# Moving operands placed elsewhere relative to their weights, and four joints between stages, in a two-block transformer kernel

## The chip, the cores and the metric

The kernel runs on one core of a Trainium2 chip. The time is that of one launch, in device microseconds (us). Engines are named as in the profile: PE is TensorE (matmuls), PEld its weight loads, DVE is VectorE, ACT is ScalarE, POOL is GpSimd, SP is the engine that issues most transfers (DMAs).

## What is computed

Two transformer blocks in a row on 256 tokens of width 2048, all in float32. Cut to the products that matter here:

```
# first block
p  = rms_norm(h) @ w_in                      # RWKV and sparse attention read p
h += concat(y_rwkv, y_att) @ w_mix_out
h += cross_attention(rms_norm(h) @ w_q, rms_norm(mem) @ w_kv) @ w_o
h += square(relu(rms_norm(h) @ w_up)) @ w_down          # w_up: 2048 x 8192
# second block, with 16 meta tokens ahead
h += mixer(rms_norm(rms_norm(h)) @ w_in_2) @ w_out_2
q  = rms_norm(h) @ w_query_2                 # picks 128 of 16384 experts per token, gates g
h += (g * gelu(rms_norm(h) @ peer_u.T)) @ peer_v        # peer_u, peer_v: 16384 x 2048
```

## The kernel before, in words

**Float32 in three products.** Every weight arrives as a tile `raw` of 128 x 1024 (512 KB, eight blocks of 128 x 128; `half`). ACT copies it to a rounded `whi` (L276, 128 x 512 a time) and DVE subtracts that to give the rest, `wlo` (L261). Each block then takes three matmuls (`linear`, `mm` at L255) into one PSUM tile `plin`: `whi` with the high half of the activations, `whi` with the low half, `wlo` with the high half. The weight block is the stationary operand, which PE loads (one load for each matmul); the activations are the moving operand, 256 columns wide. A column of output takes 16 such blocks, 48 matmuls; `evac` takes it out of PSUM.

**Names of the moving operands.** `xh`/`xl` are the normed input, in the products of w_in, w_kvc and w_mix; `uh`/`ul` the squared MLP activations, in w_down; `ph`/`pl` the pairs made by `pair`, in most other products (w_qc, w_up, w_in2, w_out2, the query and peer_u); `oh`/`ol` the attention output, in w_oc. In peer_v the roles turn: the gated activations `wh`/`wl` are stationary (128 x 128 of them at a time) and `whi`/`wlo` move, 512 columns, into eight PSUM tiles `o` that add up over all 128 groups of experts (`experts_out`).

**Stages, in order:** w_in (with the streams of RWKV and sparse attention driven between its blocks), w_kvc, w_mix, w_qc, w_oc, then w_up and w_down by turns in four parts, w_in2 (with the second block's attention streams), w_out2, the query and its top-k, peer_u, peer_v.

**What sets the order.** A scheduler places the instructions by priority; `half` is marked high priority, and `keep_in_program_order` pins DMAs on SP in program order. At a norm, PE sums squares with a vector of ones (`pcs`), DVE takes the inverse root (`rsv`, `rsh`, `ldr`, `rst`), and PE spreads it to all partitions (`pbc`). `load_norm` (L426) does the first of these and calls `inv_rms` at its end. In w_oc, `norm_tile` (L1107) splits each new column of `h` into `ph` (ACT) and `pl` (DVE), and POOL squares it (`sqt`) and adds it to `acc`. In `experts_out`, group j needs `g<-gd`, a DMA of the gates from the scattered table, then POOL's product with the activations `A`, then `wh` on ACT and `wl` on DVE.

Of the kernel before, what the change touches and what calls it, by code (L numbers as in the profile page):

```python
# [8 lines left out]
F32 = mybir.dt.float32  # L9
# [3 lines left out]
AF = mybir.ActivationFunctionType  # L13
OP = mybir.AluOpType
# [107 lines left out]
NCOL_IN = len(W_COLS)  # L122
# [61 lines left out]
def _layout(inp):  # L184
    a = {k: np.asarray(v) for k, v in inp.items()}
    o = {}
    o["x"] = _tT(a["x"][0])
    o["mem"] = _tT(a["mem"][0])
    o["pos"] = np.ascontiguousarray(a["positions"].reshape(1, S))
    o["vecs"] = _vecs(a)  # L190
    cc = _const_arrays()
    o["ident"] = np.ascontiguousarray(cc["ident"])
    o["iota"] = np.ascontiguousarray(cc["iota"])
    o["consts_a"] = np.ascontiguousarray(np.concatenate([cc[n] for n in CA], 1))
    o["dups"] = np.ascontiguousarray(np.concatenate([cc["dup"], cc["rdup"]], 1)[:64])
# [12 lines left out]
    fl = np.concatenate([w2[:, 7168:], w2[:, 7168:], np.zeros((D, 112), w2.dtype)], 1)  # L208
    qkv = w2[:, :6144].reshape(D, 2, 3, 8, 128).transpose(0, 1, 3, 2, 4).reshape(D, 6144)
    o["w_in2"] = _blocks(np.concatenate([qkv[:, :3072], fl, qkv[:, 3072:], w2[:, 6144:7168]], 1))  # L210
    o["w_out2"] = _blocks(a["w_out_2"][0])
    o["w_pq"] = _blocks(a["peer_w_query_2"][0])
    o["keys"] = np.ascontiguousarray(a["peer_sub_keys_2"][0].reshape(16, NKEY, 128).transpose(2, 0, 1))
    u = a["peer_u_2"][0].reshape(NKEY, NKEY, KT, 128)
    o["pu"] = np.ascontiguousarray(
        u.transpose(1, 3, 2, 0).reshape(NKEY, 128, 2, 8, 128).transpose(0, 2, 1, 3, 4)).reshape(2 * NKEY, 128, 8, 128)
    v = a["peer_v_2"][0].reshape(NKEY, NKEY, 2, 1024)
    o["pv"] = np.ascontiguousarray(v.transpose(1, 2, 0, 3)).reshape(2 * NKEY, 128, 8, 128)
    return o
# [25 lines left out]
class Kernel:  # L245
# [180 lines left out]
    def load_norm(self, src, gain, xh, xl, dst, eps, acc, w, tiles):  # L426

        nc = self.nc
        ts = []
        for q in range(4):  # L430
            t = tiles(q)
            with self.tc.high_priority():
                self.tc.keep_in_program_order(nc.sync.dma_start(t, src[:, 4 * q:4 * q + 4]))
            ts.append(t)
            if q < 2:
                self.ahead.append(self.half(w[len(self.ahead)], True))
            for k in range(4):
                self.split(xh[:, 4 * q + k], xl[:, 4 * q + k], t[:, k], self.v(gain, 4 * q + k))
            if q:
                self.squares(ts[q - 1], acc, q == 1, q == 1)  # L440
        with self.tc.high_priority():
            self.tc.keep_in_program_order(nc.sync.dma_start(self.ident, self.io["ident"]))
        self.squares(ts[3], acc, False)
        self.inv_rms(dst, acc, eps)

    def squares(self, t, acc, first, pool=False):

# [9 lines left out]

    def inv_rms(self, dst, acc, eps):
        r = self.small("ldr")
        with self.tc.high_priority():  # L460
            p = self.colsum([acc[:, 0], acc[:, 1]], S)
            self.rsqrt(r, p[:, 0:2], 1.0 / D, eps)
            self.bcast(dst, r, S)

    def block1(self, c0):
        nc, tc = self.nc, self.tc
# [4 lines left out]
        xp = self.pool("xa", 1, xstack)  # L471
        yp = self.pool("yp", 1, xstack)
        ctx = ExitStack()
        cp = self.pool("ca", 1, ctx)
        ph = self.pool("pa", 1, ctx)
        ca = cp.tile([128, wid], F32, name="ca")
        C = {n: ca[:, o:o + w] for n, (o, w) in off.items()}
        self.C = C
        xh = xp.tile([128, KT, S], F32R, name="xh", tag="xh")
        xl = xp.tile([128, KT, S], F32R, name="xl", tag="xl")  # L480
        rx = ph.tile([128, S], F32, name="rx")
# [63 lines left out]

        def evac(c, p):
            kind, g, q = KIND[c]
            if kind == "dsa":
                self.dsa_evac(g, p)
            elif kind == "rwkv":  # L550
                w, j = divmod(q, 2)
# [6 lines left out]
                shift(c, p, cur["AR"][:, j, 1] if w == 0 else cur["KV"[w - 1]][:, j])  # L558
                if q == 5:
                    rs.append(self.rwkv_group(g, cur["AR"], cur["K"], cur["V"], fr))  # L560
            elif g == 0:
                self.first = shift(c, p, L)
                self.act(th, L[0:64], AF.Tanh)
                ds.append(loads())
                ds.append(low_rank())
                ds.append(self.tables())
            elif g == 1:
                shift(c, p, M)
                self.act(sM[64:96], M[64:96], AF.Sigmoid)
                ds.append(self.dsa_ki())  # L570
            else:
                shift(c, p, XG)
                self.act(XG, XG, AF.Sigmoid)
# [8 lines left out]
        self.ds = (ds, ds2)  # L582

        def dense():
            yield from self.linear(self.io["w_in"], 0, NCOL_IN, KT, xh, xl, S, evac, more=(2,))
            rm = ph.tile([128, S], F32, name="rm")
            kv = self.kv = kvp.tile([128, 8, S], F32, name="kv", tag="kv")

# [16 lines left out]
                    self.squares(tile(c), xacc, c == 0)  # L605

            yield from self.linear(self.io["w_kvc"], 0, 8, KT, xh, xl, S, kv_evac)
            self.inv_rms(rm, xacc, 1e-5)
            for c in range(8):
                self.gtt(kv[:, c], kv[:, c], rm, OP.mult)  # L610

# [506 lines left out]
            self.gtt(acc, acc, t, OP.add)  # L1118

    def rstd(self, acc, dst, eps, dim=D):  # L1120
        p = self.colsum([acc], S)
        r = self.small("rr")
        self.rsqrt(r, p[:, 0:2], 1.0 / dim, eps)
        self.bcast(dst, r, S)
        return r
# [39 lines left out]
    def cross(self, cp, cxh, cxl, rc):  # L1165
# [48 lines left out]

        self.drive(self.linear(self.io["w_qc"], 0, 4, KT, cxh, cxl, S, query), todo, 1, flush=False)
        self.mxh, self.mxl = self.pair(self.xb)
        acc = wk.tile([128, S], F32, name="acc2", tag="acc", bufs=2)

        def out(c, p):
            self.vtt(h[:, c], p, h[:, c], OP.add)  # L1220
            self.norm_tile(c, h[:, c], "norm_mlp", self.mxh[:, c, 0:S], self.mxl[:, c, 0:S], acc, wk)


        first = [self.plin.tile([128, 512], F32, name="plin", tag="plin") for _ in range(2)] + [self.ps("pc"), self.ps("pc")]
# [23 lines left out]
            out(c, first[c][:, 0:S])  # L1248
        self.lin(self.io["w_oc"], 2, KT - 4, 4, oh, ol, S, out, c0=4)
        self.rm = wk.tile([128, S], F32, name="rmlp", tag="rc", bufs=2)  # L1250
        self.rstd(acc, self.rm, 1e-5)

    def mlp(self, up):
        nc, h, wk = self.nc, self.h, self.wk
        U = {}
        g12 = wk.tile([128, KT], F32, name="g12")
        o1, o2 = self.vec["norm_final"][0], self.vec["norm_mix_2"][0]
        self.vtt(g12, self.vecs[:, o1:o1 + KT], self.vecs[:, o2:o2 + KT], OP.mult)
# [54 lines left out]
        p1, p2 = self.colsum([acc1], S), self.colsum([acc2], S)
        r1, m, r2 = self.small("r1"), self.small("m2"), self.small("r2")
        self.rsqrt(r1, p1[:, 0:2], 1.0 / D, 1e-5)
        self.vtt(m, r1, r1, OP.mult)
        self.vtt(m, m, p2[:, 0:2], OP.mult)
        self.rsqrt(r2, m, 1.0 / D, 1e-6)
        self.vtt(r2, r2, r1, OP.mult)
        self.bcast(self.r12[:, NMETA:], r2, S)  # L1320
        r1b = wk.tile([128, S], F32, name="r1b", tag="rc", bufs=2)
        self.bcast(r1b, r1, S)
        for c in range(KT):
            self.gtt(h[:, c], h[:, c], r1b, OP.mult)

    def meta_tokens(self):

# [20 lines left out]
    def block2(self):  # L1348
# [8 lines left out]
        nc.sync.dma_start(ca, self.io["consts_b"])  # L1357
        C = self.C = {n: ca[:, o:o + w] for n, (o, w) in off.items()}
        bxh, bxl, r12 = self.bxh, self.bxl, self.r12
        rs = wk.tile([128, S], F32, name="r12s", tag="rc", bufs=2)  # L1360
        self.ts(rs, r12[:, NMETA:], 128 ** -0.5, None, OP.mult)
        gq = self.small("gq", 1)
        self.ts(gq, self.v("fox_q_gain_2", 0), 128 ** -0.5, None, OP.mult)

# [3 lines left out]
        yh, yl = self.pair(self.pool("xxb", 1, mx, side="right"))  # L1368
        acc_sb = wk.tile([128, S], F32, name="accsb", tag="acc", bufs=2)
        acc_fo = wk.tile([128, S], F32, name="accfo", tag="acc", bufs=2)  # L1370
        s0, s1 = [], []
# [157 lines left out]
        def evac(c, p):  # L1529
            if c == 24:  # L1530
                forget(p)
            elif c < 49:
                hd, w = divmod(c - (c > 24), 3)
                nn, n0 = ((S, NMETA), (SP, 0), (SP, 0))[w]
                t = cur[w] = b2.tile([128, nn], F32, name="qkv"[w] + "_", tag="qkv"[w], bufs=3)
                self.vtt(t, p, rs if c < 24 and w == 0 else r12[:, n0:], OP.mult)
# [24 lines left out]
            self.vtt(h[:, c], p, h[:, c], OP.add)  # L1561
            self.norm_tile(c, h[:, c], "norm_ffn_2", self.pxh[:, c, 0:S], self.pxl[:, c, 0:S], acc, wk)

        self.lin(self.io["w_out2"], 0, KT, KT, yh, yl, S, out)
        self.rf = self.xa.tile([128, S], F32, name="rf")
        self.rstd(acc, self.rf, 1e-6)
        mx.close()
# [192 lines left out]
    def experts_out(self, es):  # L1760
        nc, A, sp = self.nc, self.A, self.sp
        with ExitStack() as c:
# [12 lines left out]
            for j in range(NKEY):  # L1775
                w = A[j // 32][:, j % 32]
                with self.tc.high_priority():
# [4 lines left out]
                        self.tc.add_manual_dep(i.ins, x.ins.name, order if prev else sync, reason="the table is complete")  # L1782
                    prev = i
                    self.gtt(g, w, g, OP.mult)
                    wh, wl = ((sp if j == 0 else vp).tile([128, S], F32R, name=n) for n in ("wh", "wl"))
                    self.split(wh, wl, g)
                for hf in range(2):
                    hi, lo = self.half(self.io["pv"][2 * j + hf])
                    first, last = j == 0, j == NKEY - 1
                    for d in range(2):  # L1790
                        for b in range(2):
# [31 lines left out]
```

## Time and profile before

| what | value |
| --- | --- |
| time, median of 3 runs | 3501.79 us (3500.44 to 3502.34) |
| the profiled execution | 3498.64 us, its span 3496.9 us |
| TensorE's mean granted clock in it | 0.996 of full |
| PE busy | 3451.6 us (99% of the span), 28376 matmuls |
| DVE, ACT, POOL busy | 2298.9, 1762.9, 880.1 us |

The span runs from the first to the last instruction of the profiled execution. A busy engine is one with an instruction under way; matmuls overlap, so how fast they follow each other is read from their starts.

### The profile page before, as it was taken

To read this page: it belongs to the slowest core of one execution; us is meant where nothing else is said; L and a number is where in the kernel's file an instruction comes from. 1 tells how busy PE (TensorE), PEld (TensorE's weight loads), DVE (VectorE), ACT (ScalarE), POOL (GpSimd) and SP (SyncE) were. 2 spreads that over 40 slices of the span, in tenths; PEclk is the share of its full clock that TensorE was granted. 3 is DMA by queue.
4 is the path that set the end of the run, shared out by engine and by line. 5 is a ranking of instruction groups with operands and counts; after the bars stand their busy time and mean duration, and the time that the engine had idled before them with its cause. 6 is when DMAs were issued, how large, how long until landed. Compare 5 with 4: busy or idle time off the path is not lost.

```text
span 3496.9 us, 72405 instructions
## 1 busy us (share of the span) xinstructions
PE 3451.6 (99%) x28376; PEld 3240.5 (93%) x28376; DVE 2298.9 (66%) x4248; ACT 1762.9 (50%) x3187; POOL 880.1 (25%) x788
## 2 busy tenths in 40 slices
PE   8999999999999999999999999999999999999999
PEld 7899889899999999999999999999999888888887
DVE  7678767765656568656557799755555566666666
ACT  5444555554545455444445455555555455555554
POOL 2222213310101015200003002777777011111111
PEclk9999999999999999999999999999999999999999
DMA  5333435476767575544345656777777666666666
GB/s 198 113 119 128 165 124 184 148 218 192 226 190 228 185 230 183 158 145 145 121 133 176 202 180 188 185 186 186 187 187 185 206 210 213 211 213 211 210 214 194
DMA packets 230279, 635.99 MB, mean 182 GB/s; under 512 B 58320, under 2 KB 75408, under 8 KB 229552
## 3 DMA queue, kind: packets, MB, share of 16 engines
q1 hardware_dynamic: 193072, 631.22, 57.5%
q0 software_dynamic: 36864, 0.15, 2.3%
q8 instruction: 222, 3.64, 0.4%
q14 instruction: 121, 0.99, 0.1%
HBM read 610.16 MB, written 21.10 MB: 181 GB/s over the span
## 4 chain that ended last, share of the span: by engine, by line
PE 96%; DVE 2%; DMA 1%; issue 1%; ACT 0%; POOL 0%; DVEq 0%; SPq 0%; ACTq 0%; POOLq 0%
PE plin L255 68%; PE o L255 21%; PE po L255 1%; DVE wlo L261 1%; PE pfz L255 1%; PE pw L255 0%; PE pbc L255 0%; DMA hd<-ht 0%; PE pz L255 0%; PE pix L255 0%; PE pcs L255 0%; PE px L751 0%; PE pt L751 0%; DVE xl L264 0%; PE py L255 0%
## 5 line engine op out<-in xcount | busy, mean ns | idle before, releaser
L261 DVE TENSOR_TENSOR wlo<-raw,whi 128x512 fp32r<-128x512 f32 x2208 | 1602.7, 728 | 959.2 <-ACT whi L276 857.9
L276 ACT ACTIVATE whi<-raw 128x512 fp32r<-128x512 f32 x2208 | 1388.7, 630 | 1445.4 <-PE plin L255 988.5
L255 PE MATMUL plin<-ph,wlo 128*128 128x256 f32 (+1 forms) x4560 | 1290.8, 283 | 2.2 <-DVE wlo L261 2.2
L255 PE MATMUL plin<-pl,whi 128*128 128x256 f32 (+1 forms) x4560 | 1291.0, 283 | 0.0
L255 PE MATMUL plin<-ph,whi 128*128 128x256 f32 (+1 forms) x4560 | 1285.1, 282 | 1.6 <-DVE ut L261 0.7
L255 PEld LDWEIGHTS plin<-ph,wlo 128*128 128x128 f32 x4560 | 863.7, 190 | 4.5 <-DVE wlo L261 2.4
L255 PEld LDWEIGHTS plin<-ph,whi 128*128 128x128 f32 x4560 | 863.4, 189 | 3.0 <-issue 1.6
L255 PEld LDWEIGHTS plin<-pl,whi 128*128 128x128 f32 x4560 | 858.4, 188 | 1.6 <-issue 1.1
L1668 POOL DMA_INDIRECT gd<-GT,EI x256 | 414.7, 1620 | 347.5 <-DMA raw<-in_pu_dram 218.8
L255 PE MATMUL o<-wlo,wh 128*128 128x512 f32 x1024 | 405.8, 396 | 0.0
L255 PE MATMUL o<-whi,wl 128*128 128x512 f32 x1024 | 404.4, 396 | 0.0
L255 PE MATMUL plin<-xh,whi 128*128 128x256 f32 x1136 | 327.9, 289 | 9.0 <-ACT whi L276 8.4
L255 PE MATMUL plin<-xh,wlo 128*128 128x256 f32 x1136 | 327.4, 289 | 4.1 <-DVE wlo L261 3.9
L255 PE MATMUL plin<-xl,whi 128*128 128x256 f32 x1136 | 326.9, 288 | 1.7 <-DVE xl L264 1.7
L255 PE MATMUL o<-whi,wh 128*128 128x512 f32 x1024 | 323.4, 397 | 3.9 <-ACT wh L276 3.9
L255 PE MATMUL plin<-uh,wlo 128*128 128x256 f32 x1024 | 289.7, 283 | 0.0
L255 PE MATMUL plin<-ul,whi 128*128 128x256 f32 x1024 | 289.7, 283 | 0.0
L255 PE MATMUL plin<-uh,whi 128*128 128x256 f32 x1024 | 289.6, 283 | 0.0
L258 POOL TENSOR_TENSOR g<-A,g 128x256 f32<-128x256 f32 x128 | 105.8, 827 | 668.0 <-DMA g<-gd 546.1
L255 PEld LDWEIGHTS o<-whi,wh 128*128 128x128 f32 x1024 | 193.3, 189 | 50.9 <-ACT wh L276 4.1
L255 PEld LDWEIGHTS o<-wlo,wh 128*128 128x128 f32 x1024 | 193.4, 189 | 46.1
L255 PEld LDWEIGHTS o<-whi,wl 128*128 128x128 f32 x1024 | 192.2, 188 | 47.2
(563 smaller groups left out, 3520.4 us busy)
## 6 DMA issues: line engine op xcount, KB each, us to landing
raw<-in_pu_dram SPq DMA_DIRECT2D x256, 512.0 KB
raw<-in_pv_dram SPq DMA_DIRECT2D x256, 512.0 KB
raw<-in_w_in_dram SPq DMA_DIRECT2D x208, 512.0 KB
raw<-in_w_up_dram SPq DMA_DIRECT2D x128, 512.0 KB
raw<-in_w_down_dram SPq DMA_DIRECT2D x128, 512.0 KB
raw<-in_w_mix_dram SPq DMA_DIRECT2D x32, 512.0 KB
gd<-zero SPq DMA_DIRECT2D x64, 256.0 KB
raw<-in_w_out_dram SPq DMA_DIRECT2D x32, 512.0 KB
```

Source lines behind the costliest of these rows:

```text
L255: self.nc.tensor.matmul(out, l, r, start=start, stop=stop)
L258: self.nc.gpsimd.tensor_tensor(out, a, b, op=op)
L261: return self.nc.vector.tensor_tensor(out, a, b, op=op)
L276: return self.nc.scalar.activation(out, a, AF.Copy, **kw)
L1668: i = self.nc.gpsimd.indirect_dma_start(self.gd, bass.IndirectOffsetOnAxis(self.EI[tb][:, s:s + 1], 0), self.GT[tb][:, s:s + 1], None, com ...
```

## The change

**Pads.** Three tiles that nobody writes or reads: `xpad` (64 bytes in each partition) ahead of `xh`/`xl`, `upad` (64 bytes) ahead of `uh`/`ul`, `vpad` (480 bytes) ahead of `wh`/`wl` in peer_v. In the built program the start of `xh` in a partition goes from byte 60256 to 60320, that of `uh` from 54112 to 54176, and that of `wh` from 192896 to 193376 (the first `wh`/`wl`, of j = 0, stand in another pool and are not moved). The blocks of `whi` start at byte 35680 and every 512 bytes after it, since a block is 128 floats wide; `wlo` lies a multiple of 512 further. So the moving operand's start less the weights' start, counted modulo 512 (called its place below), goes from 0 to 64 for `xh`/`xl` and `uh`/`ul`. In peer_v, moving less stationary goes from 480 to 0. The `ph`/`pl` tiles have rows of 1088 bytes, twice 512 and 64, so that the 16 rows of one column of output stand at all eight multiples of 64 in turn, before and after.

**Joints.** (1) At the start, `load_norm` no longer ends with the inverse root; the first three columns of w_in stay in PSUM until the third is done, and then the root is taken and all three are evacuated. (2) In w_oc, ACT squares four columns at once (`hsq`, 128 x 1024) and POOL adds 128 x 512 at a time, where POOL did eight 128 x 256 operations. (3) The end of the MLP becomes a stream of the second block's schedule. (4) w_out2 begins with four columns at once, block row by block row, as its weights are laid out anew. And in `experts_out` the loads of peer_v's first weights are pinned behind the first `g<-gd`.

```diff
 def load_norm(...):
         self.squares(ts[3], acc, False)
-        self.inv_rms(dst, acc, eps)
...
+        xp.tile([128, 16], F32, name="xpad")
         xh = xp.tile([128, KT, S], F32R, name="xh", tag="xh")
...
         def evac(c, p):
             kind, g, q = KIND[c]
-            if kind == "dsa":
+            if c < 3:
+                early.append((c, p))
+                if c == 2:
+                    self.inv_rms(rx, xacc, 1e-5)
+                    for e in early:
+                        lead(*e)
+            elif kind == "dsa":
...
-            yield from self.linear(self.io["w_in"], 0, NCOL_IN, KT, xh, xl, S, evac, more=(2,))
+            yield from self.linear(self.io["w_in"], 0, NCOL_IN, KT, xh, xl, S, evac, more=(2, 3))
...
         def out(c, p):
             self.vtt(h[:, c], p, h[:, c], OP.add)
-            self.norm_tile(c, h[:, c], "norm_mlp", self.mxh[:, c, 0:S], self.mxl[:, c, 0:S], acc, wk)
+            self.split(self.mxh[:, c, 0:S], self.mxl[:, c, 0:S], h[:, c], self.v("norm_mlp", c))
+            if c % 4 == 3:
+                t = cp.tile([128, 4, S], F32, name="hsq", tag="hsq", bufs=2)
+                self.act(t, h[:, c - 3:c + 1], AF.Square)
+                if c == 3:
+                    self.gtt(acc, t[:, 0:2], t[:, 2:4], OP.add)
+                else:
+                    self.gtt(t[:, 0:2], t[:, 0:2], t[:, 2:4], OP.add)
+                    self.gtt(acc, acc, t[:, 0:2], OP.add)
...
     def mlp(self, up):
+        up.tile([128, 16], F32, name="upad")
...
+        def tail():
             p1, p2 = self.colsum([acc1], S), self.colsum([acc2], S)
...
+            yield
             self.bcast(self.r12[:, NMETA:], r2, S)
...
+        self.tail = tail()
...
-        self.lin(self.io["w_out2"], 0, KT, KT, yh, yl, S, out)
+        p = [self.plin.tile([128, 512], F32, name="plin", tag="plin") for _ in range(2)] + [self.ps("pc"), self.ps("pc")]
+        for k in range(KT):
+            if k % 2 == 0:
+                w = self.half(self.io["w_out2"][k // 2])
+            for c in range(4):
+                hi, lo = (self.block(x, 4 * (k % 2) + c) for x in w)
...
+        for c in range(4):
+            out(c, p[c][:, 0:S])
+        self.lin(self.io["w_out2"], 8, KT - 4, KT, yh, yl, S, out, c0=4)
...
+                    if j == 0:
+                        vp.tile([128, 120], F32, name="vpad", bufs=1)
                     wh, wl = ((sp if j == 0 else vp).tile([128, S], F32R, name=n) for n in ("wh", "wl"))
...
-                    hi, lo = self.half(self.io["pv"][2 * j + hf])
+                    hi, lo = self.half(self.io["pv"][2 * j + hf], j == 0)
```

At the start, DVE's order, before: the chain of the inverse root (`rsv` to the last `ldr`) with two weight splits within it.

```order
L261 TENSOR_TENSOR wlo<-raw,whi 128x512 x2
L270 TENSOR_SCALAR rsv<-pcs 128x2
L268 TENSOR_SCALAR rsh<-rsv 128x2
L270 TENSOR_SCALAR ldr<-rsh 128x2
L261 TENSOR_TENSOR rst<-ldr 128x2
L261 TENSOR_TENSOR wlo<-raw,whi 128x512
L264 SCALAR_TENSOR_TENSOR rst<-rst,rsv 128x2
L261 TENSOR_TENSOR wlo<-raw,whi 128x512
L264 SCALAR_TENSOR_TENSOR ldr<-rst,ldr 128x2
L261 TENSOR_TENSOR rst<-ldr 128x2
```

And after:

```order
L262 TENSOR_TENSOR wlo<-raw,whi 128x512 x8
L271 TENSOR_SCALAR rsv<-pcs 128x2
L269 TENSOR_SCALAR rsh<-rsv 128x2
L271 TENSOR_SCALAR ldr<-rsh 128x2
L262 TENSOR_TENSOR rst<-ldr 128x2
L265 SCALAR_TENSOR_TENSOR rst<-rst,rsv 128x2
L265 SCALAR_TENSOR_TENSOR ldr<-rst,ldr 128x2
L262 TENSOR_TENSOR rst<-ldr 128x2
```

The two weight splits now stand ahead of the chain. On PE the four `pcs` and the two `pbc` stay next to each other, behind 144 matmuls of w_in where it was 96.

In w_oc, POOL's order, before: squares and sums of one column each (`acc_9108` is the sum).

```order
L258 TENSOR_TENSOR acc_9108<-h 128x256
L258 TENSOR_TENSOR sqt<-h 128x256 x2
L258 TENSOR_TENSOR acc_9108<-acc_9108,sqt 128x256 x2
L258 TENSOR_TENSOR sqt<-h 128x256
L258 TENSOR_TENSOR acc_9108<-acc_9108,sqt 128x256
```

And after, all of it:

```order
L259 TENSOR_TENSOR acc_9109<-hsq 128x512
L259 TENSOR_TENSOR hsq<-hsq 128x512
L259 TENSOR_TENSOR acc_9109<-acc_9109,hsq 128x512
L259 TENSOR_TENSOR hsq<-hsq 128x512
L259 TENSOR_TENSOR acc_9109<-acc_9109,hsq 128x512
L259 TENSOR_TENSOR hsq<-hsq 128x512
L259 TENSOR_TENSOR acc_9109<-acc_9109,hsq 128x512
```

31 operations of 256 columns became 7 of 512.

Between peer_u and peer_v, ACT's order, before (`A` is the activation of a group of experts, the last of peer_u's work):

```order
L273 ACTIVATE A_34249<-et 128x256
L276 ACTIVATE whi<-raw 128x512 x4
L273 ACTIVATE A_34249<-et 128x256
L276 ACTIVATE wh<-g 128x256 x3
L276 ACTIVATE whi<-raw 128x512 x7
L276 ACTIVATE wh<-g 128x256
```

And after:

```order
L277 ACTIVATE whi<-raw 128x512 x4
L274 ACTIVATE A_34222<-et 128x256 x2
L277 ACTIVATE wh<-g 128x256
L277 ACTIVATE whi<-raw 128x512 x4
L277 ACTIVATE wh<-g 128x256
L277 ACTIVATE whi<-raw 128x512
L277 ACTIVATE wh<-g 128x256
```

The four `whi` that stood between the last two `A` were peer_v's; they now stand behind the last `A` and the first `wh`. On SP the first `g<-gd` now stands ahead of all loads of peer_v; it stood behind five of them.

## Rows read from the trace of the kernel before

**Rows 1.** The page, part 1: busy time, share, instructions.

```profile
PE 3451.6 (99%) x28376; PEld 3240.5 (93%) x28376; DVE 2298.9 (66%) x4248; ACT 1762.9 (50%) x3187; POOL 880.1 (25%) x788
```

**Rows 2.** The critical chain, longest pieces: start, length, engine, tile written, line, instructions.

```profile
534.96 73.75 PE plin L255 x613
693.83 718.85 PE plin L255 x6030
...
2044.97 721.14 PE plin L255 x6095
2772.92 718.91 PE o L255 x3070
```

**Rows 3.** The page, part 5: count, busy, mean ns; idle before, releaser.

```profile
L276 ACT ACTIVATE whi<-raw 128x512 fp32r<-128x512 f32 x2208 | 1388.7, 630 | 1445.4 <-PE plin L255 988.5
...
L255 PE MATMUL plin<-xh,whi 128*128 128x256 f32 x1136 | 327.9, 289 | 9.0 <-ACT whi L276 8.4
...
L255 PE MATMUL plin<-uh,whi 128*128 128x256 f32 x1024 | 289.6, 283 | 0.0
```

**Rows 4.** Timeline of PE in w_down: the first start and the fifteenth after it.

```profile
789.59 0.28 PE L255 MATMUL plin<-uh,whi 128*128 128x256 f32 x1
...
791.39 0.28 PE L255 MATMUL plin<-uh,whi 128*128 128x256 f32 x1
```

**Rows 5.** Timeline of PE in peer_u: the first start and the fifteenth after it.

```profile
2744.52 0.28 PE L255 MATMUL plin<-pl,whi 128*128 128x256 f32 x1
...
2746.29 0.28 PE L255 MATMUL plin<-pl,whi 128*128 128x256 f32 x1
```

**Rows 6.** Timeline of PE in peer_v: the first start and the ninth after it.

```profile
2999.79 0.40 PE L255 MATMUL o<-wlo,wh 128*128 128x512 f32 x1
...
3001.89 0.40 PE L255 MATMUL o<-whi,wl 128*128 128x512 f32 x1
```

**Rows 7.** Windows, peer_v's start: PE, PEld, DVE, ACT, POOL busy; granted clock; DMA share, GB/s.

```profile
2772.90:2777.80 4.90, 4.88 (x12) 3.86 (x13) 1.58 (x3) 0.83 (x2) 1.07 (x2) 0.50 1.02 420
```

**Rows 8.** Critical chain at the start: one of two splits, and the broadcast.

```profile
28.21 0.69 DVE wlo L261
...
30.87 1.22 PE pbc L255 x4
```

**Rows 9.** Windows in w_oc, columns as in rows 7.

```profile
650.00:670.00 20.00, 17.36 (x119) 16.17 (x120) 20.00 (x32) 9.91 (x19) 17.66 (x21) 0.91 0.42 132
```

**Rows 10.** Groups of instructions in w_oc, 640 to 672 us: count, busy, mean ns.

```profile
L261 DVE TENSOR_TENSOR wlo<-raw,whi 128x512 fp32r<-128x512 f32 x15 | 15.3, 1029 | 0.0
...
L258 POOL TENSOR_TENSOR acc<-acc,sqt 128x256 f32<-128x256 f32 x13 | 12.8, 983 | 0.6
L258 POOL TENSOR_TENSOR sqt<-h 128x256 f32<-128x256 f32 x14 | 12.7, 907 | 1.8 <-DVE h L261 1.8
...
L264 DVE SCALAR_TENSOR_TENSOR pl<-h,vecs,ph 128x256 fp32r<-128x256 f32 x14 | 9.5, 682 | 0.0
...
L261 DVE TENSOR_TENSOR h<-plin,h 128x256 f32<-128x256 f32 x14 | 5.7, 412 | 0.6 <-PE plin L255 0.6
```

**Rows 11.** What PE waited for: us in all, times, longest.

```profile
PE plin L255 <- DVE wlo L261: 6.1, 5, 2.2
PE plin L255 <- DVE h L261: 4.2, 7, 2.6
PE o L255 <- ACT wh L276: 3.9, 1, 3.9
PE pbc L255 <- DVE ldr L264: 3.4, 1, 3.4
PE pbc L255 <- DVE r L261: 2.5, 1, 2.5
```

**Rows 12.** DVE's timeline at the end of w_in2: start, length, form, count.

```profile
1836.16 6.13 DVE L264 SCALAR_TENSOR_TENSOR fo<-fo,vecs,rmg 128x256 f32<-128x256 f32 x8
1842.22 0.68 DVE L261 TENSOR_TENSOR wlo<-raw,whi 128x512 fp32r<-128x512 f32 x1
```

**Rows 13.** The critical chain ahead of peer_v.

```profile
2768.21 3.24 DMA g<-gd
...
2772.45 0.42 ACT wh L276
```

More of the change, by code (lines that the diff above doesn't have):

```diff
@@ L210, in _layout @@
     o["w_in2"] = _blocks(np.concatenate([qkv[:, :3072], fl, qkv[:, 3072:], w2[:, 6144:7168]], 1))
-    o["w_out2"] = _blocks(a["w_out_2"][0])
+    o["w_out2"] = np.concatenate([_blocks(a["w_out_2"][0][:, :512].reshape(KT, 128, 4, 128).transpose(0, 2, 1, 3)
+                                          .reshape(KT * 4 * 128, 128)), _blocks(a["w_out_2"][0][:, 512:])])
     o["w_pq"] = _blocks(a["peer_w_query_2"][0])
@@ L459, in inv_rms @@
         r = self.small("ldr")
[L460 to L463, printed above, removed]
+        p = self.colsum([acc[:, 0], acc[:, 1]], S)
+        self.rsqrt(r, p[:, 0:2], 1.0 / D, eps)
+        self.bcast(dst, r, S)
     def block1(self, c0):
@@ L560, in evac, with lead @@
                     rs.append(self.rwkv_group(g, cur["AR"], cur["K"], cur["V"], fr))
-            elif g == 0:
+        early = []
+        def lead(g, p):
+            c = g
+            if g == 0:
                 self.first = shift(c, p, L)
@@ L607, in dense @@
             yield from self.linear(self.io["w_kvc"], 0, 8, KT, xh, xl, S, kv_evac)
-            self.inv_rms(rm, xacc, 1e-5)
+            with tc.high_priority():
+                self.inv_rms(rm, xacc, 1e-5)
             for c in range(8):
@@ L1120, in rstd @@
     def rstd(self, acc, dst, eps, dim=D):
-        p = self.colsum([acc], S)
+        p = self.colsum(acc if isinstance(acc, list) else [acc], S)
         r = self.small("rr")
@@ L1216, in cross @@
         self.mxh, self.mxl = self.pair(self.xb)
-        acc = wk.tile([128, S], F32, name="acc2", tag="acc", bufs=2)
+        acc = wk.tile([128, 2, S], F32, name="acc2", tag="acc2")
         def out(c, p):
             self.vtt(h[:, c], p, h[:, c], OP.add)
-            self.norm_tile(c, h[:, c], "norm_mlp", self.mxh[:, c, 0:S], self.mxl[:, c, 0:S], acc, wk)
+            self.split(self.mxh[:, c, 0:S], self.mxl[:, c, 0:S], h[:, c], self.v("norm_mlp", c))
[7 more added lines that the diff above has]
+                    self.gtt(acc, acc, t[:, 0:2], OP.add)
         first = [self.plin.tile([128, 512], F32, name="plin", tag="plin") for _ in range(2)] + [self.ps("pc"), self.ps("pc")]
@@ L1250, in cross @@
         self.rm = wk.tile([128, S], F32, name="rmlp", tag="rc", bufs=2)
-        self.rstd(acc, self.rm, 1e-5)
+        self.rstd([acc[:, 0], acc[:, 1]], self.rm, 1e-5)
     def mlp(self, up):
@@ L1311, in mlp @@
                 up_cols(g + 1, 1, 15)
[L1313 to L1324, printed above, removed]
+        def tail():
+            p1, p2 = self.colsum([acc1], S), self.colsum([acc2], S)
+            r1, m, r2 = self.small("r1"), self.small("m2"), self.small("r2")
+            self.rsqrt(r1, p1[:, 0:2], 1.0 / D, 1e-5)
+            self.vtt(m, r1, r1, OP.mult)
+            self.vtt(m, m, p2[:, 0:2], OP.mult)
+            self.rsqrt(r2, m, 1.0 / D, 1e-6)
+            self.vtt(r2, r2, r1, OP.mult)
+            yield
+            self.bcast(self.r12[:, NMETA:], r2, S)
+            self.rs = wk.tile([128, S], F32, name="r12s", tag="rc", bufs=2)
+            self.ts(self.rs, self.r12[:, NMETA:], 128 ** -0.5, None, OP.mult)
+            r1b = wk.tile([128, S], F32, name="r1b", tag="rc", bufs=2)
+            self.bcast(r1b, r1, S)
+            for c in range(KT):
+                self.gtt(h[:, c], h[:, c], r1b, OP.mult)
+        self.tail = tail()
     def meta_tokens(self):
@@ L1370, in block2 @@
         acc_fo = wk.tile([128, S], F32, name="accfo", tag="acc", bufs=2)
-        s0, s1 = [], []
+        s0, s1 = [self.tail], []
         NB = [(0, 128), (128, 128), (256, 16)]
@@ L1535, in evac @@
                 t = cur[w] = b2.tile([128, nn], F32, name="qkv"[w] + "_", tag="qkv"[w], bufs=3)
-                self.vtt(t, p, rs if c < 24 and w == 0 else r12[:, n0:], OP.mult)
+                self.vtt(t, p, self.rs if c < 24 and w == 0 else r12[:, n0:], OP.mult)
                 if w == 2:
@@ L1562, in out @@
             self.norm_tile(c, h[:, c], "norm_ffn_2", self.pxh[:, c, 0:S], self.pxl[:, c, 0:S], acc, wk)
-        self.lin(self.io["w_out2"], 0, KT, KT, yh, yl, S, out)
+        p = [self.plin.tile([128, 512], F32, name="plin", tag="plin") for _ in range(2)] + [self.ps("pc"), self.ps("pc")]
[4 more added lines that the diff above has]
+                hi, lo = (self.block(x, 4 * (k % 2) + c) for x in w)
+                o = p[c][:, 0:S]
+                self.mm(o, hi, yh[:, k, 0:S], k == 0, False)
+                self.mm(o, hi, yl[:, k, 0:S], False, False)
+                self.mm(o, lo, yh[:, k, 0:S], False, k == KT - 1)
+        for c in range(4):
+            out(c, p[c][:, 0:S])
+        self.lin(self.io["w_out2"], 8, KT - 4, KT, yh, yl, S, out, c0=4)
         self.rf = self.xa.tile([128, S], F32, name="rf")
```

2 lines of the change are left out of this document (removed).

## The prediction

> **What bounds the kernel now.** I read the page's busy times first. PE is busy for 3451.6 of 3496.9 us [rows 1], so two things can change the time: the rhythm in which matmuls follow each other, and the few places where PE stands still. The chain that ended last says where the rhythm counts: its four longest pieces [rows 2] are all PE, and they hold 15,808 matmuls in 2232.7 us. PE stands still for 45 us in all [rows 1], and the waits that the joints could touch are short [rows 11].
>
> Then the rhythm of each operand, as length over count in the chain and as starts in the timeline. `xh`/`xl` (w_mix): 73.75 / 613 = 120.3 ns. `uh`/`ul`: fifteen starts in 1.80 us, 120.0 ns [rows 4]. `ph`/`pl`: fifteen in 1.77 us, 118.0 ns [rows 5], and 721.14 / 6095 = 118.3 ns over the long piece [rows 2]. The long piece from 693.83 us mixes `ph` and `uh` and gives 119.2, between them. `wh`/`wl` in peer_v: nine starts in 2.10 us, 233.3 ns for 512 columns [rows 6]. The reader is to see that the same matmul, 256 columns with one load each, takes 120 ns from one tile and 118.3 from another, with the same granted clock.
>
> How much of that is column time? Behind the pause ahead of peer_v the granted clock is 0.50, that is 1.2 GHz, and twelve rows fill 4.9 us [rows 7], 408 ns each, or 445 if one of the twelve only hangs over the edge: 512 columns at 1.2 GHz would be 427. So I take a column at one cycle with nothing over, an estimate. At 2.4 GHz that is 106.7 ns for 256 columns and 213.3 for 512. Over it stand 13.3 ns (`uh`), 11.6 (`ph`) and 20.0 (peer_v) a matmul. Something adds to each, and not the same for all.
>
> **Pads of xh/xl and uh/ul.** These two stand at place 0 for every matmul; `ph` takes all eight places in turn and is faster. That the place is what differs is my inference. If place 0 costs 120.0 inside the `ph` rotation too, and I count places by quarters of 256 bytes (so that two of the eight are at 0), the other three quarters average (4 x 118.3 - 120.0) / 3 = 117.7, and place 64 is one of them. The gain is 2.2 to 2.3 ns a matmul. The counts are 3 x 1136 for `xh`/`xl` and 3 x 1024 for `uh`/`ul` [rows 3], 6480 together; nearly all stand in stretches without a wait, so I count them all: 6480 x 2.24 = **-14.5 us**. From one side the bound is 0 (the place is not the cause: `ph` rotates, the others don't, and a rotation alone might be what helps). From the other, if three quarters cost 120 and 64 alone is fast, 64 takes 473.2 - 360 = 113.2 ns, and the gain is 6.8 x 6480 = 44 us. It may also be a slow place: at 122 ns the pads cost 13 us. I take the average of the three, since no row singles out 64.
>
> **Pad of wh/wl.** The place goes from 480, just short of 512, to 0. Both ends come from `uh`, the row at place 0. If what place 0 costs is paid per weight load, peer_v has one for each matmul as `uh` has [rows 1], the excess falls from 20.0 to 13.3, and 3072 x 6.7 = 20 us are gained. If it is paid per column, 512 columns pay twice 13.3, the matmul takes 240 ns, and 20 us are lost. The nearer row is `uh`'s with its one load a matmul, so I lean to a gain and take half: **-10 us**, with both ends kept. ACT, DVE and the DMAs stay away from the end in either case: DVE is busy for 66% and ACT for 50% of the span [rows 1].
>
> Here the Trainium skill speaks against the change. Its page "SBUF — State Buffer", section "SBUF: two separate sides", says that within the engine side only the port pair that VectorE and GpSimd share causes contention, and that PE never waits on anyone. By that, where an operand stands could not matter, both pad terms are 0, and only the joints are left. The trace does not sit easily with it: 120.0 against 118.3 ns from the same instruction. It is the rival "pads idle" below.
>
> **Joint at the start.** PE waits 3.4 us for `ldr` once [rows 11]. Two weight splits stand inside the chain of the root, one of 0.69 us [rows 8] and one a little shorter; after the change they stand ahead of it, while the rest of the chain and its place between `pcs` and `pbc` remain. So **-1.3 us**; bounds 0 (DVE reaches the chain later, as 16 splits now stand ahead) and -3.4 (the whole wait). Three evacuations come together behind it and hold up DVE's next splits, +2 at worst; the weights for the fourth column are split by then, which covers 48 matmuls, 5.8 us.
>
> **Joint in w_oc.** From 650 to 670 us DVE is busy without a gap, POOL for 17.66 of 20 and PE runs 119 rows [rows 9], about ten columns, 2.0 us each, where 12 matmuls at 120 ns would need 1.44. POOL needs 983 + 907 ns = 1.89 us a column, DVE 1029 + 682 + 412 ns = 2.12 us a column, whose four blocks of w_oc are one split [rows 10]. The split takes 0.69 elsewhere [rows 8], so it is stretched by half here while POOL is busy all the time. After the change POOL has two operations of 512 columns for four columns; even at twice 0.98 us each that is 0.98 a column, and half of the time beside it is gone. DVE then needs 0.69 + 0.68 + 0.41 = 1.78 a column if only the split recovers, 1.56 if `pl` recovers in the same ratio. I take 1.6 to 1.7, so 0.3 us less for each of the twelve columns behind the first four, against 1.9 to 2.0 now: **-3.3 us**; bounds -1.3 and -5.4. ACT gets the square as new work: 1024 elements for four columns, at 0.63 us for 512 [rows 3] some 0.3 us a column, on top of 1.0 (9.91 us for ten columns [rows 9]), still under 1.6. POOL's ready time moves from `sqt` to the square, so `pcs` comes 12 matmuls later; PE fills that with w_up.
>
> **Joints that stay as they are.** The MLP's end: PE waits 2.5 us for `r` [rows 11], which hangs on the same chain; what moves is behind it. **0**, at most -2.5. w_out2: the wait of 2.2 us for `wlo` [rows 11] is in w_in2's last columns, where the split stands on DVE behind eight `fo` (6.13 us) [rows 12]; that order is unchanged. The four-column beginning gives the last heads' operands more time, for which no wait shows now, and lets four evacuations meet at once (0.41 us each [rows 10]). **0**, between -2.2 and +0.8.
>
> **Joint ahead of peer_v.** PE waits 3.9 us for `wh` [rows 11]. The first `g<-gd` is issued at 2768.21, behind five loads of peer_v on SP, lands 3.24 us later, and `wh` ends at 2772.87 [rows 13]. Issued ahead of these loads it is early, and what is late next is ACT: peer_v's first `whi` stands behind the last `A`. PE ended peer_u at about 2769.05 (2772.92 less 3.87); `et` on DVE and `A` on ACT, taken as 0.42 each like `wh` [rows 13], `wh` 0.42 and `whi` 0.63 [rows 3], with some 0.05 between each, end at 2771.1. So **-1.8 us**; bounds 0 and -3.9. The half clock of [rows 7] may go with the pause, another 2.4 us at most; I leave it.
>
> **Sum.** -14.5 - 10 - 1.3 - 3.3 - 1.8 = -30.9 us. The profiled execution took 3498.64 (span 3496.9 and 1.7 around it), so 3467.7; the median of the runs is 3.15 above the profiled one, so **3470.9 us**. About 0.2% (7 us) is what a measurement of this kernel can tell from no change.
>
> **Rivals.**
> *Pads idle.* The rotation, not the place, makes `ph` faster, or the difference lies in how blocks change. For it: no row shows one fixed place against another. Only the joints remain, -4 to -10: about 3495, on the border between faster and the same. 17 in 100.
> *Large gain.* 64 is better than the average of its quarters (about -25), the load rule holds in full for peer_v (-20), and the joints give -8: 3449. For it: the excess over column time is large, 13 to 20 ns. 15 in 100.
> *peer_v loses.* `xh` and `uh` gain their 14.5, but 0 is a slow place for 512 columns (+7 to +20): 3488 to 3501. For it: place 0 is just the one on which the slow 256-column operands stand. 16 in 100, half of it within 0.2%.
> *Slower.* What costs is nearness of the two starts: 64 is as near as 0, so `xh`/`uh` gain nothing, and peer_v, moved onto 0, pays per column, up to 240 ns: +20.5 - 6.4 = +14, 3516. It decides from 237.7 ns on in peer_v: 233.3, and 4.4 more, since 6.4 us of joints and 7 us of margin are 13.4 us over 3072 matmuls. For it: 480 is already close to 512 and has the largest excess. Against: per column that excess is the smallest, 20.0 / 512. 12 in 100.
>
> **How the numbers follow.** The forecast has 40 in 100, its own range 3460 to 3482. Faster: 40 + 15, half of 17 and half of 16, 72; the same: the other halves, 16; slower: 12. The range of 8 in 10 goes from 3446 (within the large gain) to 3502 (the upper end of peer_v's loss); what is left out is the slower case and the lower part of the large gain.
>
> **What would show it.** In the profile after: `plin<-uh` starts 117.7 ns apart where they were 120.0, w_mix's long piece at 118 a matmul, peer_v's long piece nearer 230 than 234; `ph` unchanged at 118.3; in w_oc more than 119 rows in 20 us and a split near 0.7; PE's wait for `ldr` near 2.1 us, for `wh` or `whi` near 2.1. A `uh` rhythm still at 120.0 would show the first step wrong, a peer_v rhythm above 234 the second. I would be wrong altogether if a place's cost had nothing to do with its quarter.

## The result, and the profile after

The changed kernel took 3458.4 us (median of 4 runs, 3457.15 to 3459.34) where the kernel before took 3502.07 (4 runs); the ratio is 0.9876, 95% interval 0.9859 to 0.9893. Forecast were 3470.9 us and a range of 3446 to 3502; the time lies below the narrower 3460 to 3482 that went with the forecast alone. The gain, 43.7 us between the medians and 39.3 between the profiled executions (3498.64 and 3459.34), is larger than the 30.9 of the sum.

The page after, part 1, answers to [rows 1]: PE is busy for 37 us less with four matmuls more, and its share is still 99%.

```profile
PE 3414.2 (99%) x28380; PEld 3223.2 (93%) x28380; DVE 2292.6 (66%) x4248; ACT 1766.2 (51%) x3191; POOL 864.8 (25%) x764
```

PE's timeline after, in w_down and in peer_v; the rows answer to [rows 4, 6], first start and fifteenth after it, first and ninth.

```profile
789.57 0.28 PE L256 MATMUL plin<-uh,wlo 128*128 128x256 f32 x1
...
791.34 0.28 PE L256 MATMUL plin<-uh,wlo 128*128 128x256 f32 x1
...
2999.81 0.39 PE L256 MATMUL o<-wlo,wh 128*128 128x512 f32 x1
...
3001.85 0.39 PE L256 MATMUL o<-whi,wl 128*128 128x512 f32 x1
```

Fifteen starts of `uh` now take 1.77 us, 118.0 ns each where it was 120.0; nine of peer_v take 2.04 us, 226.7 ns where it was 233.3. The chain shows the same for all of peer_v, 718.91 us before [rows 2]:

```profile
2754.05 697.91 PE o L256 x3070
```

The starts of the stages on PE (first matmul of each, from the timelines) give the ledger:

| stage | starts before | starts after | gained within it |
| --- | --- | --- | --- |
| w_in, w_kvc, w_mix | 8.09 | 7.84 | 3.9 |
| w_qc | 603.94 | 599.83 | 0.0 |
| w_oc | 633.53 | 629.42 | 3.2 |
| w_up, w_down in parts | 670.73 | 663.44 | 7.9 |
| w_in2 to peer_u | 1407.90 | 1392.69 | 3.7 |
| peer_v, to the end of the span | 2772.92 | 2754.05 | 20.9 |
| end | 3496.9 | 3457.1 | |

With 0.25 us from the earlier start that makes the 39.8 us between the spans. In w_up and w_down, 6.8 of the 7.9 fall into the four stretches of w_down (92.15 us each before, 90.45 after).

The joints. Windows in w_oc after, the same 20 us as [rows 9], and the groups that answer to [rows 10]:

```profile
650.00:670.00 20.00, 17.93 (x147) 17.41 (x146) 19.02 (x32) 13.74 (x24) 8.78 (x6) 1.00 0.47 152
```

```profile
L262 DVE TENSOR_TENSOR wlo<-raw,whi 128x512 fp32r<-128x512 f32 x15 | 11.5, 776 | 0.0
...
L265 DVE SCALAR_TENSOR_TENSOR pl<-h,vecs,ph 128x256 fp32r<-128x256 f32 x14 | 9.3, 667 | 0.0
...
L274 ACT ACTIVATE hsq<-h 128x1024 f32<-128x1024 f32 x3 | 3.1, 1044 | 0.0
L259 POOL TENSOR_TENSOR acc<-acc,hsq 128x512 f32<-128x512 f32 x2 | 3.0, 1488 | 0.2
```

147 matmuls where there were 119, some of them already w_up's; POOL is down from 17.66 us to 8.78, and the split from 1029 ns to 776, while `pl` takes 667 where it took 682.

What PE waited for, after, against [rows 11]:

```profile
PE plin L256 <- DVE h L262: 3.5, 6, 1.3
PE pbc L256 <- DVE ldr L265: 2.8, 1, 2.8
PE pbc L256 <- DVE r L262: 2.5, 1, 2.5
...
PE o L256 <- ACT whi L277: 1.8, 1, 1.8
```

The wait ahead of peer_v is shorter by 2.1 us and is now for `whi`, as forecast. The wait for `ldr` lost 0.6. The MLP's end waits as long as before.

### The profile page after: what moved, and what is told of

Read it like the earlier page. It is cut to its first block, busy times and chain, and to the rows that moved or that the text cites. A ratio compares the mean times of both kernels' runs of the same rounds, so it can differ in the third digit from the quotient of the medians.

```text
span 3457.1 us, 72390 instructions
## 1 busy us (share of the span) xinstructions
PE 3414.2 (99%) x28380; PEld 3223.2 (93%) x28380; DVE 2292.6 (66%) x4248; ACT 1766.2 (51%) x3191; POOL 864.8 (25%) x764
## 5 line engine op out<-in xcount | busy, mean ns | idle before, releaser
L256 PE MATMUL o<-whi,wh 128*128 128x512 f32 x1024 | 315.1, 390 | 1.8 <-ACT whi L277 1.8
```

The costliest lines, as they stand in the source:

```text
L256: self.nc.tensor.matmul(out, l, r, start=start, stop=stop)
```

## Experiments

**Pads alone, joints alone.** The kernel before with the three pads, and the changed kernel without them:

```diff
+        xp.tile([128, 16], F32, name="xpad")
...
+        up.tile([128, 16], F32, name="upad")
...
+                    if j == 0:
+                        vp.tile([128, 120], F32, name="vpad", bufs=1)
```

> The kernel before with the three pads alone, no joint. Theory (the pads do their work whatever the joints do): uh matmuls 117.7 ns apart, peer_v 226.7, together 7 + 7 + 20.5 us, so some 34 us under the kernel before. Rival (part of the gain of peer_v or of xh comes only with the joints, which change when loads arrive): under 28 us.

> The changed kernel without its three pads. Theory: uh 120.0 and peer_v 233.3 ns as before, and only the joints remain: w_oc -4.3, the MLP's end -1.5, ahead of peer_v -2.1, the start +1, together -6 to -8 us. Rival (the joints give more than their own stages show, for example by the clock): 10 us or more.

Pads alone: ratio 0.991 (0.9893 to 0.9926), 3467.58 us against 3499.92, so 32 us less. Joints alone: 0.9978 (0.9969 to 0.9988), 3491.45 us, 8.5 us less, a little above the 6 to 8 expected and under the rival's 10. So the first theory stands in the time and the second nearly, and the two parts add up to about the whole change, 41 of 44 us. Not so inside the first stage: w_qc starts at 602.31 with the pads alone, at 603.80 with the joints alone, at 599.83 with both, 603.94 before. (Two kernels without either, the one before and the one with everything moved below, lie 1.0 us apart in that stage, 595.85 and 596.87, so differences of this size are weak.)

w_oc, from its first matmul to w_up's first, lasts 37.20 us before, 37.19 with the pads alone, 34.03 with the joints alone and 34.02 with both: this gain belongs to the joint. In peer_v the joints alone give something too, at the old place:

```profile
2764.40 716.66 PE o L256 x3070
```

```profile
2764.40:2769.40 5.00, 5.00 (x21) 3.97 (x22) 4.44 (x8) 3.39 (x7) 0.00 (x0) 1.00 0.92 369
```

The rhythm is that of before (2144 matmuls from 2800 to 3300 us in both kernels), but the granted clock is 1.00 in the first five us of peer_v, with 21 matmuls, where it was 0.50 with twelve [rows 7]. That makes the piece 2.25 us shorter than the 718.91 of before. The three kernels without the joint show 0.50 to 0.56 there, behind a pause of 3.9 to 4.6 us. Of the nine with it, behind a pause of 1.8, five show 1.00; four, the changed kernel among them (0.66 in the five us from 2754), run a part of the time at the lower level.

**Everything moved, nothing relative.**

```diff
+        per.tile([128, 16], F32, name="wpad")
         self.ident = per.tile([128, 128], F32, name="ident")
```

> The kernel before with one unused tile of 64 bytes ahead of everything: weights, xh, uh and wh all start 64 bytes later, their places relative to each other stay 0, 0 and 480. Theory (the place relative to the weights counts): uh 120.0 ns, peer_v 233.3, no change of time within 2 us. Rival (the moving operand's own address counts): uh near 117.7 as in the changed kernel, and peer_v off 233.3.

3496.69 us in one run, against 3499.92: 3.2 less where up to 2 was expected, but within the 13 runs of the kernel before (3496.58 to 3502.08). Timeline of w_down (fifteen starts) and the chain in this kernel:

```profile
785.52 0.28 PE L255 MATMUL plin<-uh,whi 128*128 128x256 f32 x1
...
787.32 0.28 PE L255 MATMUL plin<-uh,whi 128*128 128x256 f32 x1
```

```profile
2770.86 719.04 PE o L255 x3070
```

120.0 ns and 719.04 us: the operand's own address, moved by the same 64 bytes as in the changed kernel, does nothing. Its place relative to the weights does it. For peer_v, whose pad is of 480 bytes, a shift by 64 is the weaker test.

**Other places.** The changed kernel with other pads; as an example the first of four:

```diff
-        xp.tile([128, 16], F32, name="xpad")
+        xp.tile([128, 32], F32, name="xpad")
-        up.tile([128, 16], F32, name="upad")
+        up.tile([128, 48], F32, name="upad")
-                        vp.tile([128, 120], F32, name="vpad", bufs=1)
+                        vp.tile([128, 104], F32, name="vpad", bufs=1)
```

> The changed kernel with other pads: xh at place 128, uh at 192, peer_v at 64. Theory (a place's cost is paid per weight load, the same for 256 and 512 columns): peer_v at 64 has the excess of uh at 64, 117.7 - 106.7 = 11.0 ns, so 224.3 ns a matmul, 7 us less in peer_v; uh at 192 between 117 and 120. Rival (peer_v has a place of its own, 0 is its best): 226.7 ns or more at 64.

> The changed kernel with xh at place 256, uh at 320, peer_v at 128. Theory (places repeat every 256 bytes, as counted in quarters): xh 120.0 ns as at 0, uh 117.8 as at 64; peer_v not below 226.7. Rival (they repeat every 512 only): xh and uh have values of their own, such that the mean over eight places still meets the 118.3 of the rotating operands.

> The changed kernel with xh at place 32, uh at 448, peer_v at 256. Theory (places repeat every 256 bytes): uh 113.3 ns as at 192, peer_v 226.7 as at 0, xh between 117.3 and 120. Rival (every 512 only): uh far from 113.3, peer_v far from 226.7.

> The changed kernel with xh at place 96, uh at 160, peer_v at 96. Theory (rhythms come in whole steps of 16 cycles of 2.4 GHz, 6.67 ns, or mixes of these over the three matmuls of a block): uh one of 113.3, 115.6, 117.8, 120.0; peer_v one of 226.7, 228.9, 231.1, 233.3. Rival (the rhythm goes evenly with the place): values in between.

Timeline of w_down and the chain with `uh` at 192 and peer_v at 64:

```profile
785.57 0.28 PE L256 MATMUL plin<-ul,whi 128*128 128x256 f32 x1
...
787.27 0.28 PE L256 MATMUL plin<-ul,whi 128*128 128x256 f32 x1
```

```profile
2743.10 704.67 PE o L256 x3070
```

Fifteen starts in 1.70 us: 113.3 ns, which no row of before had shown for one place and which is under the 117 to 120 expected. Peer_v is slower at 64 than at 0, so a place's cost per load is not the same for 256 and 512 columns, and that theory falls. With `uh` at 448 and peer_v at 256:

```profile
785.61 0.28 PE L256 MATMUL plin<-uh,whi 128*128 128x256 f32 x1
...
787.31 0.28 PE L256 MATMUL plin<-uh,whi 128*128 128x256 f32 x1
```

```profile
2742.85 696.35 PE o L256 x3070
```

113.3 ns again, and 696.35 us, as at place 0 but for the clock at peer_v's start (1.00 in its first five us here, 0.66 in the changed kernel; from 2800 to 3300 us the two have 2207 and 2208 matmuls): places repeat every 256 bytes. The others confirm it and fill the table (peer_v by its chain piece of 3070 matmuls and by the matmuls from 2800 to 3300 us, `uh` by fifteen starts or by a stretch of w_down, 768 matmuls: 90.45 us at 64, 90.11 at 160; `xh` by the matmuls of w_mix from 545 to 585 us, at 64 and 192 in the first kernel that had the place):

| place (modulo 256) | 0 | 32 | 64 | 96 | 128 | 160 | 192 | 224 |
| --- | --- | --- | --- | --- | --- | --- | --- | --- |
| 256 columns (`uh`), ns | 120.0 | | 117.8 | | | 117.3 | 113.3 | |
| 256 columns (`xh`), matmuls in 40 us | 336 | 346 | 342 | 336 | 339 | | 342 | |
| 512 columns (peer_v), us | 697.9 | 716.7 | 704.7 | 718.2 | 713.8 | | 716.7 | 718.9 |
| 512 columns (peer_v), matmuls in 500 us | 2208 | 2144 | 2187 | 2145 | 2153 | | 2145 | 2144 |

The pieces in us hold the clock at peer_v's start as well, so they differ by up to 2.3 us at the same rhythm. By the counts 32, 96, 192 and 224 are one rhythm, 233.3 ns, and 128 is 232.4:

```profile
2800.00:3300.00 500.00, 500.00 (x2144) 402.52 (x2144) 314.60 (x447) 253.25 (x446) 73.64 (x90) 1.00 0.67 211
```

```profile
2800.00:3300.00 500.00, 500.00 (x2145) 402.20 (x2144) 312.68 (x447) 253.77 (x447) 72.79 (x90) 1.00 0.67 212
```

The first is the kernel before (224), the second peer_v at 96.

The windows that give `uh` at 320 (the same as 64) and at 160, 790 to 840 us of these two kernels:

```profile
790.00:840.00 50.00, 50.00 (x427) 50.00 (x427) 28.07 (x44) 22.65 (x36) 0.00 (x0) 1.00 0.59 184
```

```profile
790.00:840.00 50.00, 50.00 (x429) 50.00 (x428) 28.22 (x45) 22.66 (x36) 0.00 (x0) 1.00 0.60 189
```

Such a count takes in those that hang over the edges: with everything moved, at 120.0 ns, it is 419 where 417 fit. `xh` at 256 had 335 matmuls in the w_mix window, as at 0 (336 before). At 32 it had 346, 116.7 ns from start to start, where 117.3 to 120 was expected; at 64 and 192 other kernels showed another count (last section). 117.3 is none of the four values that I had listed for 160, so the guess that only a block's three matmuls mix was wrong; five in a row, three slow and two fast, would give that mean.

**Every operand at its best place.** `uh`, `xh` and the `ph` pairs, but that of w_in2, at 192; the pairs in rows of 1024 bytes so that the place stays fixed; peer_v first at 192, then at 0.

```diff
-    def pair(self, pool):
-        return pool.tile([128, KT, SP], F32R, name="ph", tag="ph"), pool.tile([128, KT, SP], F32R, name="pl", tag="pl")
+    def pair(self, pool, off=None):
+        t = pool.tile([128, KT, SP], F32R, name="ph", tag="ph"), pool.tile([128, KT, SP], F32R, name="pl", tag="pl")
+        if off is None:
+            return t
+        return tuple(x.rearrange("p a b -> p (a b)")[:, off:off + KT * S].rearrange("p (a b) -> p a b", b=S) for x in t)
...
-        self.mxh, self.mxl = self.pair(self.xb)
+        self.mxh, self.mxl = self.pair(self.xb, 48)
...
-        self.pxh, self.pxl = self.pair(self.xa)
+        self.pxh, self.pxl = self.pair(self.xa, 16)
```

> The changed kernel with xh and uh at place 192, and the ph pairs of w_qc, w_up, w_out2, the query and peer_u laid in rows of 1024 bytes at one fixed place, 192 (in w_in2 they keep rotating); peer_v at 192. Theory (the place makes the rhythm, for any operand): ph 113.3 ns where it was 118.3, so 10,900 matmuls x 4.9 = 53 us less, uh and xh 6480 x 4.4 = 28 us less; with peer_v no slower than 229, about 3380 us. Rival (rotation makes ph faster than a fixed place by itself, and uh at 192 is fast for a reason of w_down): ph not under 118, time near 3440.

> The changed kernel with every 256-column operand at the place that was fastest for it (xh, uh, and the ph pairs but that of w_in2 at 192, in rows of 1024 bytes) and peer_v at 0. Theory (stages add up, each with its own rhythm): the one with peer_v at 192, 3405.0 us of span, less 3072 x 6.7 ns = 20.5 us: a span near 3384.5, some 2% under the changed kernel. Rival (faster matmuls meet another limit, such as the weight loads from memory): over 3395.

With peer_v at 192: 3407.2 us in one run. Timeline in peer_u, fifteen starts, against [rows 5], and the windows in w_mix:

```profile
2300.53 0.28 PE L256 MATMUL plin<-ph,whi 128*128 128x256 f32 x1
...
2302.23 0.28 PE L256 MATMUL plin<-ph,whi 128*128 128x256 f32 x1
```

```profile
545.00:585.00 40.00, 40.00 (x342) 40.00 (x341) 31.30 (x43) 20.99 (x36) 12.13 (x16) 1.00 0.60 188
```

`ph` goes at 113.3 ns too: 192 is fast for it as for `uh`, and faster than the rotation. `xh` at 192 in the same kernel did not follow (342 matmuls, where 353 fit at 113.3 ns). That the rotation gave the mean of its places is not shown: the places of the table, with some 118.5 for 128 from `xh`, average 117.4, and `ph` had 118.3. The 3380 expected were too low by 27 us. Peer_v loses 18.8 at 192 (its piece is 716.67 us long), where the expectation had allowed for 7; and w_qc starts at 594.66, 5 us earlier than in the changed kernel and not the 15 that were counted. These are some 22 of the 27; the rest was not traced.

With peer_v at 0: 3388.28 us (median of 4), ratio to the kernel before 0.9686 (0.967 to 0.9703), against 0.9876 for the changed kernel. Windows in w_mix and the chain in this kernel:

```profile
545.00:585.00 40.00, 40.00 (x356) 40.00 (x355) 32.25 (x45) 21.86 (x37) 11.78 (x14) 1.00 0.62 196
```

```profile
2682.70 697.92 PE o L256 x3070
```

The span is 3385.8 us, 1.3 above the 3384.5 expected, and the rival's 3395 was not met. The match to the us is luck in part: against the kernel with peer_v at 192, w_mix took 2.5 us less at the same place, and the stretch from w_in2 to peer_v 3.2 more.

**The joint at the start undone.** The changed kernel with the root taken after two columns, as before (the lines of `load_norm`, `inv_rms`, `evac` and `more` of the kernel before), and peer_v at 32.

> The changed kernel with the joint at the start undone (the root taken after two columns, as before), and peer_v at place 32 (read by itself). Theory (the joint at the start gave nothing): the last matmul of w_mix ends within 1 us of the changed kernel's 599.8. Rival (it gave the 1.3 us that the prediction took): 601 or later. Peer_v at 32: between the 226.7 of place 0 and the 228.9 of 64, if the rhythm goes evenly between places.

One run, 3475.43 us, with 18.8 us lost in peer_v alone (716.66 us at 32, in the table). w_mix ended at 598.96, 0.9 us before the changed kernel, so by the letter the joint gave nothing. That doesn't settle it, because w_mix went faster here at the same place, 355 matmuls in the window of 545 to 585 us against 342:

```profile
545.00:585.00 40.00, 40.00 (x355) 40.00 (x354) 32.68 (x45) 22.23 (x38) 13.37 (x16) 1.00 0.62 197
```

Up to the first of w_mix's 768 matmuls the joint does show: it starts 490.07 us behind the first of w_in in the changed kernel, 491.33 here and 492.06 with the pads alone, so 1.3 to 2.0 us, against the spread of 1.0 named above.

Peer_v at 32 was outside the 226.7 to 228.9 that an even rhythm would give; it takes as long as at 192.

## Why the prediction was right, and where its sizes were off

**xh/xl and uh/ul.** For `uh` the step was right in mechanism and size: 2.2 ns forecast, 118.0 and 117.8 measured against 120.0, 6.8 us in w_down against 3072 x 2.24 = 6.9. The shift of everything shows the mechanism as far as the prediction had it, the relative place; why a place costs what it does no run shows. The working behind it was lucky in one way: the three other quarters are not alike (117.8, 117 to 119, 113.3), and 64 happens to lie near their mean. The bound of 113.2 that the working kept for one fast quarter exists, at 192, but by coincidence: it took 120 for the other three. For `xh` the size was off: 7.6 us were counted, the three stages gained 3.9 with the joint, and the pads alone only 1.6 (603.94 to 602.31). In w_mix, where nothing but this product runs, the rhythm came (342 matmuls in 40 us against 336 before). In w_in it did not all reach the end. Windows of w_in and w_kvc, 8 to 530 us, before and with the pads alone:

```profile
8.00:530.00 522.00, 505.79 (x6955) 462.41 (x6956) 382.45 (x796) 265.67 (x524) 132.58 (x124) 0.99 0.42 140
```

```profile
8.00:530.00 522.00, 502.87 (x6960) 459.64 (x6961) 379.00 (x796) 266.83 (x525) 133.24 (x124) 0.99 0.42 140
```

PE stands still for 2.9 us more there, and so gets through only five matmuls more. All but 0.1 of that falls before 100 us:

```profile
8.00:100.00 92.00, 86.33 (x636) 80.89 (x637) 70.66 (x134) 54.90 (x101) 26.66 (x22) 0.96 0.54 187
```

```profile
8.00:100.00 92.00, 83.49 (x627) 78.23 (x628) 67.45 (x132) 55.04 (x101) 26.40 (x21) 0.96 0.54 187
```

Two waits of PE from 5 to 75 us, which the kernel before does not have, make it up in the kernel with the pads alone:

```profile
PE plin L255 <- DVE wlo L261: 1.6, 1, 1.6
...
PE pcs L255 <- POOL xacc L258: 1.3, 1, 1.3
```

The second is not the pads' doing: it is there with everything moved as well (1.2), and in no kernel with the joint at the start. What brings the first is open. The 601st matmul of `xh`/`xl` so starts 2.7 us later than before (109.33 against 106.63), and from it to the last one the pads gain 4.3 us of the 6.3 that 2808 matmuls were to give. "Nearly all stand in stretches without a wait, so I count them all" is the step that failed.

**peer_v.** The direction was right. The term was sized at -10, half of what the load rule gave; 21.0 us came (718.91 to 697.91), with the load rule's own 226.7 ns to the tenth; some 20.5 of them are rhythm, and the rest is the clock at peer_v's start, which the prediction had left out. But the rule is not why: at 64 it asked for 224.3 and got 228.9, so the match at 0 was no proof of it. Of the 12.5 us by which the median lies under the forecast, 11 are this half.

**Start.** -1.3 was forecast. The two splits did leave the chain, yet the wait fell by only 0.6, and with joints alone w_qc starts 0.1 us earlier. By the wait the term was 0.7 too large. But the wait for `xacc` above is gone as well in all eight kernels with this joint, where three of the four without it have it (the kernel before is the fourth), and beside the pads the way to w_mix is 1.3 to 2.0 us shorter. What the joint is worth lies between 0 and 2 us, and one trace of each kernel does not say where.

**w_oc.** -3.3 forecast (0.3 us for twelve columns, as written, would be 3.6), 3.2 measured. Another 1.1 us come right behind it, but not by the joint: w_up and w_down without w_down's own gain are 1.5 us shorter with the pads alone and with everything moved, which have no joint. What differs is the granted clock from 685 to 690 us, before and with the pads alone:

```profile
685.00:690.00 5.00, 4.98 (x29) 5.00 (x30) 3.74 (x14) 2.42 (x6) 1.42 (x2) 0.66 0.55 162
```

```profile
685.00:690.00 5.00, 5.00 (x44) 5.00 (x43) 3.98 (x15) 2.88 (x7) 0.25 (x1) 1.00 0.48 150
```

It is 1.00 there in the changed kernel and with everything moved too. The reason held only in part: the split recovered to 776 ns instead of 0.69 us and `pl` not at all, but POOL was out of the way. The Trainium skill's page "SBUF — State Buffer", section "SBUF: two separate sides", has VectorE and GpSimd share a port pair; the split's 1029 against 776 ns with a quieter POOL agrees with it.

**MLP's end.** 0 was forecast and 1.5 us came, for which the joint is not needed. The eight `pbc` behind the same wait, in the kernel before, after, with pads alone, and with everything moved (no joint in the last two):

```profile
L255 PE MATMUL pbc<-ident,r x8: 421/421/551, 1423.1 to 1424.8; 128*128 128x128 f32 x8
```

```profile
L256 PE MATMUL pbc<-ident,r x8: 275/275/347, 1407.9 to 1408.8; 128*128 128x128 f32 x8
```

```profile
L255 PE MATMUL pbc<-ident,r x8: 421/421/553, 1413.2 to 1414.9; 128*128 128x128 f32 x8
```

```profile
L255 PE MATMUL pbc<-ident,r x8: 275/275/347, 1422.3 to 1423.1; 128*128 128x128 f32 x8
```

After the same stall of 2.5 us TensorE goes on at its lower level in two of the four and at its upper in the others (granted clock 0.66 in the five us from 1423 before, 1.00 in those from 1408 after), with or without the joint. (Of the nine kernels with it, eight have a median of 275 and the one with `uh` at 320 has 316; whether the joint makes the upper level likelier these runs do not tell.) **w_out2**: 0 as forecast, its matmuls begin and end with the same lead of 16.7 us.

**Ahead of peer_v.** -1.8 forecast, 2.1 measured (the pause 3.9 to 1.8), by the mechanism named: the gates are early, ACT's `A`, `wh` and `whi` are last.

**The rule against the change.** The same section of the Trainium skill says that PE never waits on anyone. That sentence is about engines in each other's way; what the prediction drew from it, that the place of an operand could not matter, the runs refute: 113.3 to 120.0 ns for the same matmul by its two operands' places, and everything moved together changes nothing. The rival "pads idle" is out.

## What to carry to other kernels

When matmuls follow each other without a wait, read their starts for each pair of operands: if the same shape goes at different rhythms, the start of the moving tile relative to the weights, modulo 256 bytes, is worth a sweep, one place for each operand in one kernel, since the stages can be read apart. Read the rhythm in a dense stretch, away from the stage's start and its clock, and read it again in the final kernel: w_mix went at two rhythms at one place. The best place depends on the width (192 for 256 columns, 0 for 512 here), and a fixed place needs rows that are a multiple of 256 bytes. A pitch that rotates through the places gave up the best one: fixing it at 192, with `xh` and `uh` there too, took this kernel from 3458 to 3388 us, more than the change itself.

## What the runs showed that I had not expected

The rhythms sit on steps: 113.3 and 120.0 ns are 272 and 288 cycles of 2.4 GHz, 226.7 and 233.3 are 544 and 560, always 16 apart, and the means of other places lie between as mixes would. That they are mixes is argued, not shown: at 64 with the pads alone, every start in w_down from 790 to 840 us is 117 to 119 ns behind the one before it, and none 113 or 120.

A place does not fix the rhythm by itself. The two kernels with all at 192 are the same up to peer_v, and their w_mix went at 342 and 356 matmuls in the same 40 us, 117.8 and 113.3 ns from start to start; at place 64 it was 342 (changed kernel) and 355 (start undone). In these windows a dense stretch stays in one of the two; what decides is open. `uh` showed no such pair: 117.8 at 64 in each of four kernels, 113.3 at 192 in four others.
